# Modulation vectors as sums along rows on VectorE, and four pairs of tiles in the first k loop

## The chip, the cores and the metric

The kernel runs on one core of one Trainium2 chip. The metric is the device time of one execution in microseconds (us), the median over the runs shown. TensorE (PE in the rows), VectorE (DVE), ScalarE (ACT), GpSimd (POOL) and the queue that issues the transfers (SyncE, SP) each work through a stream of their own in order and wait for each other by semaphores.

## The reference, cut to what matters

One block of a network on x of 512 tokens by 1024 features, in float32. A conditioning vector c of 1024 numbers is made into nine vectors of 1024 (shift, scale and gate of three sublayers), the modulation vectors; the sublayers use them. The full reference has a pooled and state-space mixer as its second sublayer, which the change leaves as it is.

```
mod = (silu(c) @ w_ada + b_ada).reshape(1, 3, 3, 1024)     # w_ada: 1024 x 9216
shift, scale, gate = mod[:, :, 0], mod[:, :, 1], mod[:, :, 2]
h = rmsnorm(x, norm_g[0]) * (1 + scale[:, 0]) + shift[:, 0]
x = x + 0.5 * gate[:, 0] * swiglu(h, ffn1_in, ffn1_out)     # a, b = split(h @ w_in); (silu(a) * b) @ w_out
h = rmsnorm(x, norm_g[1]) * (1 + scale[:, 1]) + shift[:, 1]
x = x + gate[:, 1] * hybrid_mixer(h, ...)
h = rmsnorm(x, norm_g[2]) * (1 + scale[:, 2]) + shift[:, 2]
x = x + 0.5 * gate[:, 2] * swiglu(h, ffn2_in, ffn2_out)
return rmsnorm(x, final_g)
```

## The kernel before, in words

Features lie on the 128 partitions: x is 8 tiles (k = 0 to 7) of 128 features by 512 tokens. Every large product runs as three float32r matmuls (`mm3`, L312 to L314): weight and activation are each split into a rounded part and the rest (hi and lo), and hi·hi, hi·lo and lo·hi are added up in one PSUM bank. A weight unit of 128x1024 is eight 128x128 tiles. It is loaded into `w_raw`, ScalarE writes its hi part (L123, `w_hi`), and VectorE the lo part (L126, `w_lo`); five units are held split and three raw, and the splitting runs up to three units ahead of the products.

**Start.** `first_pairs` writes the order of all engines by hand. The transfers of x come first, then the constants `vec`, then the weights in the order of use. ScalarE squares the tiles of x, VectorE adds the squares (L685), TensorE sums them over the partitions (L352), eleven small steps on VectorE make the inverse root per token (L695 to L346), and TensorE spreads it over the partitions (L375, called rs). TensorE fills its idle stretches there with matmuls of ones (L672).

**First k loop.** The first `NSTART` pairs of output tiles of the first layer (three pairs, so six PSUM banks) are summed with k outermost, since the first k can start before the others are ready. Step k needs the modulated tile h[k], as hi and lo, and so scale and shift of sublayer 0 for the 128 features of tile k. They come from w_ada: `ada_load` fetches four tiles of 256 KB for a step, `ada_first` runs eight matmuls of 128x32 by 128x256 in plain float32 (L406), each of which leaves two records, ScalarE copies the rows out (L409), and `ada_turn` turns them with two transposes (L419) and adds and reduces them in three small steps on VectorE (L420 to L425). Then x·rs·gs (L515, into `tmp`), the hi part on ScalarE (L516) and the lo part on VectorE (L517) follow. For k = 0 these are L725, L730, and L731 with L732; the first matmul of the loop is L740.

**Pairs after the loop.** Each later pair is two products of 24 matmuls (k innermost), with silu and product behind them (`glu`, L605 and L607, split at L325 and L327). `ffn` runs the 22 pairs in three portions; after each portion come eight output products of one bank each, which add gate times product to x (L524).

**Other modulation vectors.** The other seven of the nine vectors are made behind the k loop by a generator, `ada_rest`, that `pump` advances six steps per pair and one per output product: 112 steps, each a multiply-add of a 128x512 tile on VectorE (L464, L466); after every eight steps `ada_row` sums over the partitions with four matmuls against ones (L486), ScalarE copies the row, and four small transfers scatter it over the partitions.

After `first_pairs`, TensorE's order is the program's, and the other engines' orders are made by a scheduler.

## Time and profile before

| | |
|---|---|
| median of 3 runs | 1163.68 us (1160.77 to 1164.01) |
| profiled execution | 1160.53 us, of which the span from first to last instruction is 1158.5 us |
| granted TensorE clock, mean over the span | 0.996 of full speed |
| TensorE busy | 1146.2 us, 99% of the span |
| VectorE busy | 629.9 us, 54% |
| ScalarE busy | 396.6 us, 34% |
| GpSimd busy | 119.3 us, 10% |
| moved by transfers | 140.17 MB |

A share is taken over the whole span. Matmuls overlap their neighbours, so a matmul's recorded length is longer than the distance to the next one; in a full stream the distance between starts is what one costs.

### The profile page before, as it was taken

To read this page: it belongs to the slowest core of one execution; us is meant where nothing else is said; L and a number is where in the kernel's file an instruction comes from. 1 tells how busy PE (TensorE), PEld (TensorE's weight loads), DVE (VectorE), ACT (ScalarE), POOL (GpSimd) and SP (SyncE) were. 2 spreads that over 40 slices of the span, in tenths; PEclk is the share of its full clock that TensorE was granted. 3 is DMA by queue.
4 is the path that set the end of the run, shared out by engine and by line. 5 is a ranking of instruction groups with operands and counts; after the bars stand their busy time and mean duration, and the time that the engine had idled before them with its cause. 6 is when DMAs were issued, how large, how long until landed. Compare 5 with 4: busy or idle time off the path is not lost.

```text
span 1158.5 us, 15066 instructions
## 1 busy us (share of the span) xinstructions
PE 1146.2 (99%) x5948; PEld 940.8 (81%) x5948; DVE 629.9 (54%) x975; ACT 396.6 (34%) x660; POOL 119.3 (10%) x122
## 2 busy tenths in 40 slices
PE   8999999999999999999999999999999999999997
PEld 6677787777877997888888878899888888888887
DVE  4567736667363666677968595563333333333334
ACT  4352222221223453454544453343321222212232
POOL 0000000000000320023112561121000000000001
PEclk9999999999999999999999999999999999999999
DMA  9585735756352411222212213440332233323312
GB/s 346 170 293 178 261 115 198 256 190 228 123 178 91 141 60 52 77 73 73 74 55 73 73 56 91 124 131 20 91 91 91 93 103 96 92 91 91 95 33 73
DMA packets 52837, 140.17 MB, mean 121 GB/s; under 512 B 7456, under 2 KB 8864, under 8 KB 52768
## 3 DMA queue, kind: packets, MB, share of 16 engines
q1 hardware_dynamic: 52768, 139.23, 37.1%
q8 instruction: 46, 0.75, 0.3%
q14 instruction: 23, 0.19, 0.1%
HBM read 137.08 MB, written 2.10 MB: 120 GB/s over the span
## 4 chain that ended last, share of the span: by engine, by line
PE 98%; DVE 1%; DMA 0%; ACT 0%; SPq 0%; issue 0%; DVEq 0%; ACTq 0%
PE ps_mm L312 24%; PE ps_mm L313 23%; PE ps_mm L314 23%; PE ps_t L314 6%; PE ps_t L313 6%; PE ps_t L312 6%; PE ps_y L965 1%; PE ps_mm L352 1%; PE ps_mm L406 1%; PE ps_t L959 1%; PE ps_y L984 1%; PE ps_mm L375 1%; PE ps_t L927 0%; DMA x<-in_x_dram 0%; PE ps_t L930 0%; PE ps_t L932 0%
## 5 line engine op out<-in xcount | busy, mean ns | idle before, releaser
L312 PE MATMUL ps_mm<-big,w_hi 128*128 128x512 f32 (+1 forms) x1192 | 454.9, 382 | 0.0
L313 PE MATMUL ps_mm<-big,w_hi 128*128 128x512 f32 (+1 forms) x1192 | 448.1, 376 | 0.1
L314 PE MATMUL ps_mm<-big,w_lo 128*128 128x512 f32 (+1 forms) x1192 | 448.0, 376 | 0.0
L123 ACT CAST w_hi<-w_raw 128x1024 fp32r<-128x1024 f32 (+1 forms) x178 | 185.9, 1045 | 521.3 <-PE ps_mm L313 309.4
L126 DVE TENSOR_TENSOR w_lo<-w_raw,w_hi 128x1024 fp32r<-128x1024 f32 (+1 forms) x178 | 220.8, 1242 | 171.7 <-ACT w_hi L123 160.6
L312 PEld LDWEIGHTS ps_mm<-big,w_hi 128*128 128x128 f32 x1192 | 224.1, 188 | 50.3 <-issue 8.2
L314 PEld LDWEIGHTS ps_mm<-big,w_lo 128*128 128x128 f32 x1192 | 224.1, 188 | 44.8
L313 PEld LDWEIGHTS ps_mm<-big,w_hi 128*128 128x128 f32 x1192 | 224.2, 188 | 43.6 <-issue 0.7
L314 PE MATMUL ps_t<-big,w_lo 128*128 128x512 f32 x312 | 123.4, 396 | 0.0
L312 PE MATMUL ps_t<-big,w_hi 128*128 128x512 f32 x312 | 123.4, 396 | 0.0
L313 PE MATMUL ps_t<-big,w_hi 128*128 128x512 f32 x312 | 123.4, 396 | 0.0
L524 DVE SCALAR_TENSOR_TENSOR x<-ps_mm,mod,x 128x512 f32<-128x512 f32 (+1 forms) x79 | 51.1, 648 | 127.6 <-PE ps_mm L314 127.5
L331 POOL TENSOR_TENSOR sacc<-sacc,sq 128x256 f32<-128x256 f32 (+1 forms) x30 | 28.7, 956 | 747.4 <-ACT sq L386 416.1
L607 DVE TENSOR_TENSOR tmp<-tmp,ps_t 128x512 f32<-128x512 f32 x39 | 26.8, 688 | 104.4 <-PE ps_t L314 104.4
L466 DVE SCALAR_TENSOR_TENSOR big<-big,sc 128x512 f32<-128x512 f32 x98 | 73.6, 751 | 12.6 <-DMA big<-in_ada_dram 10.1
L314 PEld LDWEIGHTS ps_t<-big,w_lo 128*128 128x128 f32 x312 | 58.6, 188 | 14.2
L313 PEld LDWEIGHTS ps_t<-big,w_hi 128*128 128x128 f32 x312 | 58.6, 188 | 14.2
L312 PEld LDWEIGHTS ps_t<-big,w_hi 128*128 128x128 f32 x312 | 58.6, 188 | 14.1
L877 DVE SCALAR_TENSOR_TENSOR big<-ps_mm,vec,big 128x511 f32<-128x511 f32 (+2 forms) x60 | 44.7, 745 | 2.2 <-ACT big L875 1.3
L325 ACT CAST big<-tmp 128x512 fp32r<-128x512 f32 (+1 forms) x66 | 36.5, 556 | 2.0 <-DVE tmp L607 1.4
L312 PE MATMUL ps_mm<-big 128*128 128x256 f32 x128 | 36.5, 286 | 0.0
L313 PE MATMUL ps_mm<-big 128*128 128x256 f32 x128 | 36.2, 283 | 0.0
(179 smaller groups left out, 891.1 us busy)
## 6 DMA issues: line engine op xcount, KB each, us to landing
w_raw<-in_ffn_in_dram SPq DMA_DIRECT2D x78, 512.0 KB, 3.5
big<-in_ada_dram SPq DMA_DIRECT2D x144, 256.0 KB, 4.8
w_raw<-in_ffn_out_dram SPq DMA_DIRECT2D x44, 512.0 KB, 3.8
w_raw<-in_w_in_dram SPq DMA_DIRECT2D x32, 512.0 KB, 3.5
w_raw<-in_w_outB_dram SPq DMA_DIRECT2D x10, 512.0 KB, 3.6
w_raw<-in_w1s_dram SPq DMA_DIRECT2D x8, 384.0 KB, 5.8
w_raw<-in_w_outA_dram SPq DMA_DIRECT2D x6, 512.0 KB, 3.9
x<-in_x_dram SPq DMA_DIRECT2D x8, 256.0 KB, 5.3
```

What stands on the lines that cost most here:

```text
L123: nc.scalar.copy(out=hi[:, :n], in_=r)
L126: nc.vector.tensor_tensor(out=lo[:, :n], in0=r, in1=hi[:, :n].bitcast(F32), op=ALU.subtract)
L312: T.matmul(o, lhsT=hi, rhs=ahi[:, s], start=first, stop=False)
L313: T.matmul(o, lhsT=hi, rhs=alo[:, s], start=False, stop=False)
L314: T.matmul(o, lhsT=lo, rhs=ahi[:, s], start=False, stop=last)
L325: self.nc.scalar.copy(out=hi[:, s], in_=src[:, :n])
L331: self.nc.gpsimd.tensor_tensor(out=acc, in0=acc, in1=q, op=ALU.add)
L352: self.nc.tensor.matmul(ps[:, at + j:at + j + 1], lhsT=acc[:, c * P - c0:(c + 1) * P - c0], rhs=self.ones[:, 0:1], start=i == 0, stop=i == ...
L466: V.scalar_tensor_tensor(out=acc, in0=ws.pop(i), scalar=self.sc[:, q:q + 1], in1=acc, op0=ALU.mult, op1=ALU.add)
L524: self.nc.vector.scalar_tensor_tensor(out=xs, in0=ps[:, :n], scalar=self.mod[:, gate, m:m + 1], in1=xs, op0=ALU.mult, op1=ALU.add)
L607: nc.vector.tensor_tensor(out=g32, in0=sa, in1=pb[:, :n], op=ALU.mult)
L877: V.scalar_tensor_tensor(out=acc[:, s:], in0=ps[:, :NT - s], scalar=tap(3 - s), in1=acc[:, s:], op0=ALU.mult, op1=ALU.add)
```

## The change

All nine modulation vectors are made in one way, without TensorE. The weights w_ada lie transposed in memory, so that a tile `row` of 128x1024 holds, for 128 output features, all 1024 weights of each. c is copied to all partitions (`cb`, 128x1024, 512 KB) and put through silu once. One call of `tensor_tensor_reduce` multiplies a row tile with `cb` and adds up along the row, starts from the bias and scales on the way, so that it leaves 128 finished numbers (`ada_sum`). Four row tiles are held (`NROW`). `ada_first`, `ada_turn` and `ada_row` are gone, and so are the small transfers of `ada_row`. `ada_rest` becomes 56 steps, three per pair and one per output product.

The k loop carries four pairs, which takes all eight PSUM banks; rs, which lay in one of them, is copied to a tile of its own (`rs_sb`) first. Its weight unit grows from 128x768 to 128x1024. In step 0 the order of the matmuls becomes hi·hi for all eight tiles, then lo·hi, then hi·lo. x is loaded, squared and added in tiles of two k. The number of `big` tiles falls from 50 to 48, and the numbers of warming matmuls change.

```diff
-NSTART = 3
+NSTART = 4
-NBIG = 50
+NBIG = 48
-PREADA = 5
-PUMPS = (6, 1)
-WARM = 22
-WARM1 = 0
-WARM2 = 3
-WARM3 = 2
+NROW = 4
+PUMPS = (3, 1)
+WARM = 24
+WARM1 = 7
+WARM2 = 4
...
+    def ada_load(self, j, k):
+        w = self.sb.tile([P, KD * P], F32, name="row", tag="row", bufs=NROW)
+        self.nc.sync.dma_start(out=w, in_=self.a["ada"][j, k])
+        return w
+
+    def ada_sum(self, j, k, w):
+        sub, typ = divmod(j, 3)
+        scale, bias, out = 1.0, self.bada[:, j, k:k + 1], self.mod[:, j, k:k + 1]
+        if typ == 1:
+            scale, bias, out = self.ng[:, sub, k:k + 1], self.gb[:, sub, k:k + 1], self.gs[:, sub, k:k + 1]
+        elif typ == 2 and sub != 1:
+            scale, bias = 0.5, self.hb[:, sub, k:k + 1]
+        self.nc.vector.tensor_tensor_reduce(out=w, in0=w, in1=self.cb, scale=scale, scalar=bias,
+                                            op0=ALU.mult, op1=ALU.add, accum_out=out)
+
+    def ada_rest(self):
+        steps = [(j, k) for j in (2, 4, 3, 5, 7, 6, 8) for k in range(KD)]
+        ws = []
+        for i, (j, k) in enumerate(steps):
+            ws += [self.ada_load(*t) for t in steps[len(ws):i + NROW]]
+            self.ada_sum(j, k, ws[i])
             yield
...
+        def load(k):
+            if k < KD:
+                rows[k] = [self.ada_load(j, k) for j in (1, 0)]
+            self.W.load(k + 1)
...
+        S.activation(out=self.cb, in_=self.cb, func=AF.Silu)
...
+        self.ada_sum(1, 0, rows[0][0])
+        warm(WARM1)
         v, y, t, u = self.root_tiles(NCHK)
...
+        rs = self.spread(y)
+        warm(WARM2)
         h = self.new_h()
+        self.ada_sum(0, 0, rows[0][1])
+        n0, rs_sb = self.tmp(), self.big()
+        V.tensor_tensor(out=n0, in0=self.x[:, 0, :], in1=rs, op=ALU.mult)
...
+        def prepare(k):
+            for j, w in zip((1, 0), rows.pop(k)):
+                self.ada_sum(j, k, w)
+            t, (hi, lo) = self.tmp(), h[k]
+            V.scalar_tensor_tensor(out=t, in0=self.x[:, k, :], scalar=self.gs[:, 0, k:k + 1], in1=rs_sb,
+                                   op0=ALU.mult, op1=ALU.mult)
+            shift = self.mod[:, 0, k:k + 1]
+            S.activation(out=hi, in_=t, func=AF.Identity, bias=shift)
+            return lambda: V.scalar_tensor_tensor(out=lo, in0=t, scalar=shift, in1=hi.bitcast(F32),
+                                                  op0=ALU.add, op1=ALU.subtract)
...
         for k in range(KD):
-            load(k + 3)
+            load(k + 2)
             ws = self.W.take(2 * NSTART)
...
+            else:
+                for w, p in zip(ws, pss):
+                    self.mm3(p, w, h[k], FULL, False, k == KD - 1)
+            if k < KD - 1:
+                rest = []
+                self.W.ensure(k + 2, lambda: rest.append(prepare(k + 1)))
+                rest[0]()
```

In the rows below the names are the program's tiles, and the line numbers are those of each kernel's own file. The first place is TensorE in step k = 1 of the loop. Before, from the modulation matmuls of a later k to the transposes of the next and the matmul behind them (`ps_mm_241` and up are the banks of the pairs):

```order
L406 MATMUL ps_mm_300<-big_201,sc32_81 32x256 x2
L312 MATMUL ps_mm_241<-big_161,w_hi_276 128x512
L313 MATMUL ps_mm_241<-big_162,w_hi_276 128x512
L314 MATMUL ps_mm_241<-big_161,w_lo_277 128x512
L312 MATMUL ps_mm_242<-big_161,w_hi_276 128x512
L313 MATMUL ps_mm_242<-big_162,w_hi_276 128x512
L314 MATMUL ps_mm_242<-big_161,w_lo_277 128x512
L419 MATMUL ps_mm_331<-vec_65,tmp_309 128x128 x2
L312 MATMUL ps_mm_243<-big_161,w_hi_276 128x512
```

The same engine in the changed kernel, from the last bank of step 1 into step 2 (`mm3` is now L310 to L312, `w_hi_284` the unit of step 2):

```order
L310 MATMUL ps_mm_213<-big_179,w_hi_244 128x512
L311 MATMUL ps_mm_213<-big_180,w_hi_244 128x512
L312 MATMUL ps_mm_213<-big_179,w_lo_245 128x512
L310 MATMUL ps_mm_206<-big_181,w_hi_284 128x512
L311 MATMUL ps_mm_206<-big_182,w_hi_284 128x512
L312 MATMUL ps_mm_206<-big_181,w_lo_285 128x512
```

The matmuls of L406 and the transposes of L419 are gone from between the steps; a step is 24 matmuls of one kind where it was 18, with ten more behind and between them.

The second place is VectorE in the loop. Before, what it does for one step:

```order
L126 TENSOR_TENSOR w_lo_277<-w_raw_193,w_hi_276 128x768
L420 TENSOR_REDUCE mod_82<-ps_mm_280 128x2
L422 SCALAR_TENSOR_TENSOR gs_83<-mod_82,vec_65,gb_111 128x1
L425 TENSOR_TENSOR mod_82<-mod_82,vec_65 128x1
L515 SCALAR_TENSOR_TENSOR tmp_286<-x_68,gs_83,ps_mm_219 128x512
L517 SCALAR_TENSOR_TENSOR big_162<-tmp_286,mod_82,big_161 128x512
```

And in the changed kernel (an ISA row of 128x1024 is the product and sum of `ada_sum`, the ISA row of 128x1 behind it reads the result out; L124 splits the weights, `w_raw_118`):

```order
L402 ISA row_114,gs_79<-row_114,cb_73,gb_142,vec_65 128x1024
L402 ISA gs_79 128x1
L402 ISA row_116,mod_78<-row_116,cb_73,vec_65 128x1024
L402 ISA mod_78 128x1
L652 SCALAR_TENSOR_TENSOR tmp_249<-x_68,gs_79,big_195 128x512
L124 TENSOR_TENSOR w_lo_245<-w_raw_118,w_hi_244 128x1024
L656 SCALAR_TENSOR_TENSOR big_180<-tmp_249,mod_78,big_179 128x512
```

Three small steps became two long ones with a read-out each; the split of the weights, a third longer, moved behind x·rs·gs.

The third place is the transfer queue at the start of the program. Before:

```order
L650 DMA x<-in_x_dram 128x512 x8
L651 DMA vec<-in_vec_dram 128x416
L395 DMA big<-in_ada_dram 128x512 x4
L103 DMA w_raw<-in_w1s_dram 128x768
L395 DMA big<-in_ada_dram 128x512 x4
```

And in the changed kernel:

```order
L569 DMA x<-in_x_dram 128x1024 x4
L571 DMA cb<-in_c_dram 128x1024
L572 DMA vec<-in_vec_dram 128x408
L391 DMA row<-in_ada_dram 128x1024 x2
L101 DMA w_raw<-in_w1s_dram 128x1024
```

`cb` stands new between x and `vec`, and the unit of weights behind the two row tiles of step 0 is larger. In the order that the scheduler makes behind the loop, 54 of the 56 sums of `ada_rest` stand between the fourth `glu` product and the twelfth behind it on VectorE; in the same stretch stand 25 splits of weight units (L124), 12 `glu` products with their lo parts, and the 8 additions to x of the first portion. The orders of VectorE, ScalarE and GpSimd in the mixer and behind it are those of before.

## Rows read from the trace of the kernel before

**Rows 1.** The page: busy time of TensorE, and the chain that ended last.

```profile
PE 1146.2 (99%) x5948; PEld 940.8 (81%) x5948; DVE 629.9 (54%) x975; ACT 396.6 (34%) x660; POOL 119.3 (10%) x122
...
PE 98%; DVE 1%; DMA 0%; ACT 0%; SPq 0%; issue 0%; DVEq 0%; ACTq 0%
```

**Rows 2.** Waits of TensorE over the span, the two longest: us, times, longest.

```profile
PE ps_mm L740 <- ACT big L730: 2.0, 1, 2.0
PE ps_mm L352 <- DVE big L685: 1.2, 1, 1.2
```

**Rows 3.** Timeline of TensorE, start and length: loop's start, its end, next pair.

```profile
19.90 0.50 PE L740 MATMUL ps_mm<-big,w_hi 128*128 128x512 f32 x1 [2.03 <-ACT big L730]
...
63.88 0.40 PE L312 MATMUL ps_mm<-big,w_hi 128*128 128x512 f32 x1
...
69.48 0.40 PE L312 MATMUL ps_t<-big,w_hi 128*128 128x512 f32 x1
...
75.08 0.40 PE L312 MATMUL ps_mm<-big,w_hi 128*128 128x512 f32 x1
```

**Rows 4.** Timeline of TensorE in step k = 1.

```profile
26.71 0.50 PE L312 MATMUL ps_mm<-big,w_hi 128*128 128x512 f32 x1
...
31.32 1.07 PE L406 MATMUL ps_mm<-big,sc 128*32 128x256 f32 x16
32.32 0.50 PE L312 MATMUL ps_mm<-big,w_hi 128*128 128x512 f32 x1
```

**Rows 5.** Line L486 over the span, and TensorE's timeline around its first call.

```profile
L486 PE MATMUL ps_y<-big,ones x112: 272/285/297, 97.6 to 351.3; 128*32 128x128 f32 x112
...
97.25 0.40 PE L314 MATMUL ps_t<-big,w_lo 128*128 128x512 f32 x1
...
97.93 0.50 PE L312 MATMUL ps_mm<-big,w_hi 128*128 128x512 f32 x1
98.27 0.40 PE L313 MATMUL ps_mm<-big,w_hi 128*128 128x512 f32 x1
```

**Rows 6.** Groups of VectorE by shape: busy us, mean ns; then its timeline, in a stretch without waits.

```profile
L126 DVE TENSOR_TENSOR w_lo<-w_raw,w_hi 128x1024 fp32r<-128x1024 f32 x170 | 213.1, 1255 | 158.5 <-ACT w_hi L123 149.1 <-PE ps_t L961 1.4
L466 DVE SCALAR_TENSOR_TENSOR big<-big,sc 128x512 f32<-128x512 f32 x98 | 73.6, 751 | 12.6 <-DMA big<-in_ada_dram 10.1
...
87.33 0.75 DVE L466 SCALAR_TENSOR_TENSOR big<-big,sc 128x512 f32<-128x512 f32 x1
87.99 1.22 DVE L126 TENSOR_TENSOR w_lo<-w_raw,w_hi 128x1024 fp32r<-128x1024 f32 x1
89.13 0.69 DVE L327 TENSOR_TENSOR big<-tmp,big 128x512 fp32r<-128x512 f32 x1
89.73 0.75 DVE L466 SCALAR_TENSOR_TENSOR big<-big,sc 128x512 f32<-128x512 f32 x1
```

**Rows 7.** Timelines of VectorE and ScalarE at the start: first and last root step, step 0.

```profile
12.81 0.16 DVE L695 TENSOR_SCALAR root<-ps_mm 128x4 f32<-128x4 f32 x1 [0.98 <-PE ps_mm L352]
...
14.79 0.16 DVE L346 SCALAR_TENSOR_TENSOR root<-root 128x4 f32<-128x4 f32 x1
...
18.31 0.68 DVE L725 TENSOR_TENSOR tmp<-x,ps_mm 128x512 f32<-128x512 f32 x1
...
20.67 0.49 DVE L732 TENSOR_SCALAR big<-tmp,mod 128x512 fp32r<-128x512 f32 x1
...
19.03 0.82 ACT L730 ACTIVATE big<-tmp,mod,gs 128x512 fp32r<-128x512 f32 x1 [1.95 <-DVE tmp L725]
```

**Rows 8.** Stretches: length, busy time by engine, granted clock, DMA share, GB/s.

```profile
2.00:8.00 6.00, 6.00 (x39) 6.00 (x38) 0.69 (x1) 2.72 (x6) 0.00 (x0) 1.00 0.97 292
8.00:18.00 10.00, 7.80 (x58) 5.80 (x56) 5.46 (x19) 4.08 (x9) 0.00 (x0) 0.83 1.05 395
13.00:16.00 3.00, 3.00 (x22) 1.51 (x22) 1.64 (x10) 0.03 (x1) 0.00 (x0) 0.50 1.06 396
18.00:24.00 6.00, 4.10 (x30) 2.70 (x31) 4.11 (x10) 1.93 (x3) 0.00 (x0) 1.00 1.05 390
```

## The prediction, made before the changed kernel was timed

> **What bounds the kernel now.** I read the busy times and the chain first [rows 1]: TensorE is busy for 1146.2 of 1158.5 us, and the chain of work that ended last runs through it for 98% of the span. Then its waits [rows 2]: the longest is 2.0 us, before the first matmul of the k loop, and both that are shown lie in the first 20 us. VectorE, with 54%, is waited for only there. So the time is the sum of what TensorE has to do, plus a start of some 20 us in which it waits for its first operands. What leaves TensorE's stream behind the start is gained in full, as long as no other engine becomes late for it.

> The price of a matmul is read from the distance of starts, not from its length. From 63.88 to 69.48 us a product of 24 matmuls of 128x512 runs [rows 3]: 5.60 us, or 0.2333 us each, though each is recorded with 0.40. The k loop starts at 19.90 and its last matmul is followed by the fourth pair's first at 63.88; that pair, two products, ends at 75.08. So from the loop's start to the end of pair four TensorE takes 55.18 us, of which 4 x 2 x 8 x 3 = 192 matmuls are 44.80.

> **What is removed.** A step of the loop takes from 26.71 to 32.32, 5.61 us, with 18 matmuls, 4.20 us [rows 4]. The other 1.41 us are the modulation matmuls of L406 (start to next start 1.00, and the neighbours' spacing) and the two transposes. Over the loop 43.98 - 33.60 = 10.4 us go to this and to one short wait. All of that leaves TensorE. Behind the loop `ada_row` goes: around its first call the matmul at 97.25 is followed by the next but one, not counting L486, at 98.27, 1.02 us where two spacings are 0.47 [rows 5]. That is 0.555 us a call, and 112 records at two for each of four matmuls are 14 calls: 7.8 us. It is gained whole, because TensorE has no wait in that stretch. The fourth pair's matmuls only move into the loop.

> **What VectorE gets.** The product and sum of 128x1024 is in no row. The nearest is the split of a weight unit, also two float32 streams of 1024 elements out of SBUF: 1.255 us long, and 1.14 from its start to the next one's where nothing is waited for (87.99 to 89.13) [rows 6]. The read-out is a small step; the root's small steps, each behind the last, come every 0.2 us (ten in 1.98) [rows 7]. So a sum costs at least 1.14 us, if its read-out is free, 1.34 with the read-out in sequence, 1.46 if the read-out also waits for the whole length, and at most about 2.5, if product and sum are two passes of 1.14 with a read-out. I take **1.4**, because it is one instruction with the split's operands and output. A step of the loop then holds two sums, x·rs·gs (0.66 us from start to start, as L466 at 87.33), the split 1.14 and the lo part 0.66: 2.8 + 2.46 = **5.26 us**, against 24 x 0.2333 = 5.60 for TensorE. VectorE stays ahead up to a sum of (5.60 - 2.46) / 2 = 1.57 us.

> [...]

> Behind the loop VectorE does 54 sums in a stretch with 25 splits (1.14), 12 glu products with lo parts (0.60 each, as L327 from 89.13 to 89.73) and 8 additions to x (0.66): 28.5 + 14.4 + 5.3 + 54 x 1.4 = 124 us. TensorE spends on the same stretch eight pairs of 11.20 and eight output products of 5.60, 134.4 us. The sums fit, up to 1.6 us each. What waits in VectorE's queue behind a late sum is the next split, and TensorE for that; splits run up to three units, 16.8 us of products, ahead. So the edit to `ada_rest` costs nothing under cover of that slack, and with the cover gone 54 times the excess.

> **The start.** What was ready at 19.90 is ready when? Transfers run at 292 GB/s in the stretch that brings x, later at 395 [rows 8]. At these rates the 2.10 MB of x are in at about 8.9 us. Then `cb` (0.52 MB, 1.3 us), `vec` (0.21, 0.5) and the first row tile (1.3) come, at about 12.1; the second at 13.4, the weights of step 0 at 14.8. In VectorE's order the first sum stands ahead of the root, which is queued behind it: 12.1 + 1.4 = 13.5. The eleven root steps took from 12.81 to 14.95: ready at 15.65. The second sum ends at 17.05; in its cover TensorE spreads rs. Then x·rs 0.68 and the hi part 0.82 [rows 7], with two handovers: first matmul at **18.6**. Bounds: if x too came at 395 GB/s, 1.6 us earlier, 16.9; if the first row tile lands only with the whole group behind it, at 14.8, 21.3. So the start gains 1.3 us (3.0 to -1.4).

> Step 1 then meets a late VectorE: after x·rs at 17.75 come the split (1.14), L731's and L732's successors (0.75, 0.49 [rows 7]), a constant (0.2), two sums (2.8), x·rs·gs, the split and the lo part (0.66, 1.14, 0.75). That ends at 25.65, while TensorE could take the second matmul of step 1 at 18.6 + 5.60 + 0.23 = 24.4. A wait of **1.2 us** is new. From step 2 VectorE gains 0.34 us a step. Transfers: a step needs 1.57 MB in 5.26 us, 300 GB/s, below the 395 seen, and the queue is two steps ahead; hidden.

> [...] ScalarE gets one silu of 128x1024 ahead of the first sum (about as long as a split, ready before the row tile) and the copy of rs to a tile, which the eighth bank's first matmul waits for, 1.6 us after the loop's start; both hidden. Two fewer `big` tiles: the orders in the mixer are unchanged, so nothing.

> **The sum.** Fourth pair done at 18.6 + 44.8 + 1.2 = 64.6 where it was 75.08: 10.5 us. With 7.8 from `ada_row`: **18.3 us** less. The profiled execution took 1160.5 us, its span and 2.0 around it, which gives 1142.2; the median of the runs is 3.2 higher and would give 1145.4. I say **1144**.

> **The rivals.**
> 1. *The start and the first steps eat part of it.* First matmul at 21.3 and the low clock: 18.3 - 2.7 - 1.5 = 14, so 1149 or so. For it speaks `cb` and a sum ahead of the root; against it that w_ada's tiles of step 0 were not what the old start waited for last.
> 2. *VectorE becomes the bound* (the other side). At 2.5 us a sum a step of the loop takes 5.0 + 2.46 = 7.46, 1.86 over TensorE's, seven times: 13. Two sums at the start and two in step 1: 4.4 more. Behind the loop 48.2 + 135 = 183 against 134.4 + 16.8 ahead: 32. In all 49 - 18 = 31 slower, 1193. It decides where the losses reach 18: at a sum of about 2.05 us. For it: the accumulation has no row. [...]
> 3. *In between*, a sum of 1.6 to 2.05 us: part of the gain, 1150 to 1162; at 1.8 us the loop loses 3.2, start and step 1 1.6, and the cover behind takes the rest: 1149.
> 4. *The freed time comes back as waits elsewhere*: transfers (312 GB/s in the output products, with 2 to 3 row tiles each) or a split that stands behind a sum waiting for its row. 1155 to 1165. Against it: the queue has four row tiles and splits are three units ahead.

> **How the numbers follow.** Forecast (1139 to 1148) 0.70, rival 1 0.09, rival 2 0.09, rival 3 0.07, rival 4 0.05. The range 1139 to 1153 holds the forecast, rival 1 and half of rival 3. A difference within 0.3%, 3.5 us, can't be told from none here. Faster takes the forecast, rival 1, most of 3 and some of 4: 0.86. Same: 0.04. Slower: 0.10.

> **What would show it.** In the new profile: the sum's instruction at 1.1 to 1.3 us and its read-out below 0.2; steps of the loop at 5.60 us; loop from about 18.6 to 64.6 with one wait of about 1 us in its second step; no wait of TensorE for VectorE behind it. A sum above 1.6 us, or row tiles on which VectorE waits with TensorE behind it, would make the prediction wrong.

## The result and the profile after

The changed kernel takes 1137.52 us in the median (1137.45 to 1137.97, 4 runs); before, in the same comparison, took 1163.53. The ratio is 0.978 (95% interval 0.9765 to 0.9799): 26.0 us less. The forecast of 1144 had the direction and much of the path right, but the time lies below its range (1139 to 1153), and the gain is 7.7 us larger than the sum of 18.3.

The page of the changed kernel, busy time and the chain that ended last, against [rows 1]:

```profile
PE 1126.4 (99%) x5708; PEld 937.9 (83%) x5708; DVE 635.6 (56%) x969; ACT 391.2 (34%) x632; POOL 117.3 (10%) x122
...
PE 98%; DMA 1%; DVE 1%; SPq 0%; issue 0%; DVEq 0%
```

TensorE still sets the time, with 240 records fewer. Its waits over the whole span, against [rows 2]:

```profile
PE ps_mm L350 <- DVE w_hi L615: 1.3, 1, 1.3
PE ps_mm L591 <- DVE ones L580: 1.1, 1, 1.1
PE ps_mm L373 <- DVE root L344: 0.5, 1, 0.5
```

All three lie in the start; VectorE's 72 sums of 128x1024 have brought no wait behind it. The groups of the new instruction (busy us, mean ns) answer the disputed price:

VectorE's timeline, at the start and in one step of the loop, answers to [rows 6, 7]:

```profile
11.89 1.34 DVE L402 CUSTOM_DVE_ANT_0 row<-row,cb,gb 128x1024 f32<-128x1024 f32 x1 [0.64 <-DMA row<-in_ada_dram]
13.16 0.08 DVE L402 DVE_READ_ACCUMULATOR2_ANT gs<- 128x1 f32 x1
13.16 0.16 DVE L625 TENSOR_SCALAR root<-ps_mm 128x4 f32<-128x4 f32 x1
...
15.14 0.16 DVE L344 SCALAR_TENSOR_TENSOR root<-root 128x4 f32<-128x4 f32 x1
15.22 1.28 DVE L402 CUSTOM_DVE_ANT_0 row<-row,cb,vec 128x1024 f32<-128x1024 f32 x1
...
17.47 0.69 DVE L634 TENSOR_TENSOR tmp<-x,ps_mm 128x512 f32<-128x512 f32 x1 [0.96 <-PE ps_mm L373]
...
25.41 1.34 DVE L402 CUSTOM_DVE_ANT_0 row<-row,cb,gb 128x1024 f32<-128x1024 f32 x1
26.68 0.08 DVE L402 DVE_READ_ACCUMULATOR2_ANT gs<- 128x1 f32 x1
26.68 1.28 DVE L402 CUSTOM_DVE_ANT_0 row<-row,cb,vec 128x1024 f32<-128x1024 f32 x1
...
30.35 1.33 DVE L402 CUSTOM_DVE_ANT_0 row<-row,cb,gb 128x1024 f32<-128x1024 f32 x1
```

Where the next instruction doesn't need its result, a sum is followed by it after 1.2 to 1.27 us: the read-out lies inside that. A step takes 30.35 - 25.41 = 4.94 us. TensorE's timeline in the places of [rows 3]:

```profile
19.06 2.60 PE L667 MATMUL ps_mm<-big,w_hi 128*128 128x512 f32 x8
...
25.20 0.40 PE L310 MATMUL ps_mm<-big,w_hi 128*128 128x512 f32 x1
25.55 0.50 PE L311 MATMUL ps_mm<-big,w_hi 128*128 128x512 f32 x1
...
70.21 0.40 PE L310 MATMUL ps_t<-big,w_hi 128*128 128x512 f32 x1
...
75.81 0.40 PE L310 MATMUL ps_mm<-big,w_hi 128*128 128x512 f32 x1
```

The first product behind the loop ends at 70.21 and takes as long as the second, 5.60, so the four pairs are done at 64.61, where before they were done at 75.08.

Laid side by side, equal matmuls of the two profiled executions stand 10.47 us apart there. At each of the 14 places where `ada_row` was they move 0.555 further apart, to 18.22 behind the last one (352 us in the kernel before). And then, in stretches that the change doesn't touch, the lead grows on: to about 19.0 through the mixer (800 us before) and to 22.18 through the second feed-forward layer. Stretches of 200 us: length, TensorE's busy time and records, clock, DMA share, GB/s. The kernel before:

```profile
860.00:1060.00 200.00, 200.00 (x859) 1.00 0.31 94
```

The changed kernel, in the first feed-forward layer and in the second:

```profile
100.00:300.00 200.00, 200.00 (x859) 1.00 0.56 196
860.00:1060.00 200.00, 200.00 (x867) 1.00 0.30 95
```

No wait, a granted clock of 1.00 in all three, the same instructions: yet 867 matmuls where there were 859. Between starts that is 0.2311 us against 0.2333 (mean of the distances in the stretch), 5.547 us for a product of 24 against 5.600.

### The profile page after: what moved, and what is told of

Its sections match the earlier page's. It is cut to its first block, busy times and chain, and to the rows that moved or that the text cites. A ratio compares the mean times of both kernels' runs of the same rounds, so it can differ in the third digit from the quotient of the medians.

```text
span 1136.2 us, 14273 instructions
## 1 busy us (share of the span) xinstructions
PE 1126.4 (99%) x5708; PEld 937.9 (83%) x5708; DVE 635.6 (56%) x969; ACT 391.2 (34%) x632; POOL 117.3 (10%) x122
## 4 chain that ended last, share of the span: by engine, by line
PE 98%; DMA 1%; DVE 1%; SPq 0%; issue 0%; DVEq 0%
PE ps_mm L311 24%; PE ps_mm L310 24%; PE ps_mm L312 24%; PE ps_t L311 6%; PE ps_t L312 6%; PE ps_t L310 6%; PE ps_y L887 1%; PE ps_mm L373 1%; PE ps_t L881 1%; PE ps_y L906 1%; PE ps_mm L350 1%; DMA row<-in_ada_dram 1%; PE ps_mm L667 1%; PE ps_t L849 0%; PE ps_t L854 0%; PE ps_t L852 0%
## 5 line engine op out<-in xcount | busy, mean ns | idle before, releaser
L310 PE MATMUL ps_mm<-big,w_hi 128*128 128x512 f32 (+1 forms) x1198 | 451.8, 377 | 0.0
L312 PE MATMUL ps_mm<-big,w_lo 128*128 128x512 f32 (+1 forms) x1198 | 450.0, 376 | 0.0
L121 ACT CAST w_hi<-w_raw 128x1024 fp32r<-128x1024 f32 x176 | 185.0, 1052 | 515.2 <-PE ps_mm L311 341.4
L124 DVE TENSOR_TENSOR w_lo<-w_raw,w_hi 128x1024 fp32r<-128x1024 f32 x176 | 220.2, 1252 | 169.4 <-ACT w_hi L121 159.4
L310 PEld LDWEIGHTS ps_mm<-big,w_hi 128*128 128x128 f32 x1198 | 225.1, 188 | 46.9 <-issue 2.9
L312 PEld LDWEIGHTS ps_mm<-big,w_lo 128*128 128x128 f32 x1198 | 224.9, 188 | 42.7
L311 PE MATMUL ps_t<-big,w_hi 128*128 128x512 f32 x304 | 120.2, 395 | 0.0
L312 PE MATMUL ps_t<-big,w_lo 128*128 128x512 f32 x304 | 120.1, 395 | 0.0
L310 PE MATMUL ps_t<-big,w_hi 128*128 128x512 f32 x304 | 119.0, 391 | 0.0
L310 PEld LDWEIGHTS ps_t<-big,w_hi 128*128 128x128 f32 x304 | 57.0, 188 | 14.0
L311 PEld LDWEIGHTS ps_t<-big,w_hi 128*128 128x128 f32 x304 | 57.0, 188 | 13.9
L312 PEld LDWEIGHTS ps_t<-big,w_lo 128*128 128x128 f32 x304 | 57.1, 188 | 12.7
L402 DVE CUSTOM_DVE_ANT_0 row<-row,cb,vec 128x1024 f32<-128x1024 f32 x32 | 40.3, 1279 | 2.7 <-DMA row<-in_ada_dram 2.7
L310 PE MATMUL ps_mm<-big 128*128 128x256 f32 x128 | 36.5, 285 | 0.0
```

Of the source, the lines that this page charges most:

```text
L121: nc.scalar.copy(out=hi[:, :n], in_=r)
L124: nc.vector.tensor_tensor(out=lo[:, :n], in0=r, in1=hi[:, :n].bitcast(F32), op=ALU.subtract)
L310: T.matmul(o, lhsT=hi, rhs=ahi[:, s], start=first, stop=False)
L311: T.matmul(o, lhsT=hi, rhs=alo[:, s], start=False, stop=False)
L312: T.matmul(o, lhsT=lo, rhs=ahi[:, s], start=False, stop=last)
L402: self.nc.vector.tensor_tensor_reduce(out=w, in0=w, in1=self.cb, scale=scale, scalar=bias, op0=ALU.mult, op1=ALU.add, accum_out=out)
```

## The experiments

Every run stood beside runs of the kernel before on the same chip, which took 1161.96 to 1163.32 us in the median.

**The sum's price and VectorE's cover.** Three sums per step in `prepare`; the extra one leaves the shift vector other than the reference's:

```diff
             self.ada_sum(j, k, w)
+            self.ada_sum(0, k, w)
```

> The changed kernel with three sums in place of two in each step k = 1 to 7 of the first loop; the third repeats the shift's on the tile that the second has overwritten, so shift of sublayer 0 is wrong for those tiles. My reading (VectorE is covered as long as a step of it is below TensorE's 5.60 us): a sum measured 1.24 from start to start, a step is 4.94 us, with a third one 6.18: VectorE becomes the bound, the loop's end moves from 64.6 to about 69.2, 4.6 us more than the changed kernel, 1142, and TensorE waits about 0.6 us for VectorE in each step. Rival: the steps have slack elsewhere (splits ahead), less than 2 us more.

1144.8 us (1144.11 to 1145.13), 7.3 more than the changed kernel, and more than expected: TensorE's clock fell once more, to a granted clock of 0.50 from 27.9 to 31.3 us (matmuls start 0.43 us apart there and 0.23 behind it). VectorE's steps take 6.26 us, and TensorE now waits for it inside the loop:

```profile
27.54 1.34 DVE L402 CUSTOM_DVE_ANT_0 row<-row,cb,gb 128x1024 f32<-128x1024 f32 x1
...
33.80 1.34 DVE L402 CUSTOM_DVE_ANT_0 row<-row,cb,gb 128x1024 f32<-128x1024 f32 x1
```

```profile
PE ps_mm L311 <- DVE big L657: 2.0, 5, 0.5
PE ps_mm L310 <- ACT big L656: 1.6, 2, 1.0
```

So VectorE sets the loop here, 6.26 us a step where TensorE's 24 matmuls take 5.60. From the other side, with `NSTART = 3` TensorE's step shrinks to 18 matmuls, 4.20 us:

> The changed kernel with three pairs in the k loop (a smaller unit of weights, 128x768, in it). By the prediction's count a step of VectorE is two sums of 1.24, x times rs times gs 0.66, the split 0.86 and the lo part about 0.75, 4.7 us, against 18 matmuls, 4.20 us: VectorE ends last, seven steps lose 0.45 us each and step 1 some 1.4 more, about 4.5 us: 1142. Rival (VectorE gains enough lead or the fourth pair pays it back): 1137.5.

1141.34 us (1139.73 to 1142.91), 3.8 more. VectorE's step is 4.68 us (29.37 to 34.05), and TensorE's waits again name it:

```profile
PE ps_mm L311 <- DVE big L656: 1.7, 7, 0.3
```

Behind the loop, each of the 56 sums twice (the second adds up the products, so the vectors aren't the reference's):

```diff
             self.ada_sum(j, k, ws[i])
+            self.ada_sum(j, k, ws[i])
```

> The changed kernel with each of the 56 sums behind the loop made twice, the second from the overwritten tile, so the modulation vectors of sublayers 1 and 2 and the first gate are wrong. My reading: VectorE has 134 us in the stretch and needs 48 + 54 x 1.24 = 115; with 108 sums 182, so the order, if it were kept, would cost 182 - 134 - 17 = 31 us; the scheduler may spread the sums over more pairs, since the whole first layer has 270 us, and then the price is smaller. 5 to 31 us more than the changed kernel, with waits of TensorE for splits or for the first gate. Rival: nothing (below 2 us), which would say that the sums had far more cover than I counted.

1138.17 us (1134.07 to 1138.98): nothing. The scheduler spread the sums until 276 us instead of 193; the cover is far larger than the 134 us that the prediction counted.

**What `ada_row` cost.** Its matmuls taken out of the kernel before, the copy reading `acc` instead; the sum over the partitions is left out:

```diff
-        for i in range(4):
-            nc.tensor.matmul(ps[32 * i:32 * (i + 1), 0:P], lhsT=self.ones[:, 0:32], ...)
...
-        nc.scalar.copy(out=row[:, 0:P], in_=ps[:, 0:P])
+        nc.scalar.copy(out=row[:, 0:P], in_=acc[:, 0:P])
```

> The kernel before without the 56 matmuls of ada_row: the row is copied from the accumulated tile itself, so the sum over the partitions is left out and the modulation vectors but shift and scale of sublayer 0 are wrong. My term: 7.8 us less than the kernel before, from TensorE alone, 14 calls of 0.555; the copies on ScalarE and the small transfers stay. Rival: TensorE waits elsewhere for part of it, 0 to 5 us less. By Theory R the distances in later stretches may change as well, and add up to 4 us either way; the time at the first matmul behind the last call tells the term by itself.

1156.05 us, ratio 0.9936 (0.9921 to 0.9951): 6.3 less than before by the medians. Its profiled execution started late (loop done at 66.95), which hides part of the gain. Beside `b_scratch` below, which started as late (66.69), its matmuls are 0.27 us behind at the loop's end and 7.44 ahead at the end of the program: 7.7 us gained.

**The kernel before, once more, and the start.**

> The kernel before, unchanged, profiled once more. Theory R (rhythm): the 3 us between this kernel's runs at 1160.8 and at 1163.5 are a change in the distance between matmul starts in some stretch, with the same instructions; if this execution takes about 1163.5, its profile shows some stretch in which products of 24 matmuls take more than 5.60 us or in which TensorE runs otherwise than in the first profile, and no new wait. Rival W: a wait or a late transfer at the start makes the 3 us; then the first matmul of the k loop stands 3 us after 19.9. If it takes 1160.5 the profile repeats the first within 0.3 us and nothing is told apart.

1162.19 us (1159.93 to 1163.88, 10 runs). All distances are those of the first trace; the loop starts at 20.4 instead of 19.90 and ends 2.0 us later. So what differs is neither a distance in a later stretch nor a wait, but the clock. The two executions (columns as above), first this one, then the one behind the prediction:

```profile
12.00:18.00 6.00, 5.78 (x43) 0.72 1.05 396
18.00:25.00 7.00, 4.97 (x28) 0.76 1.05 392
```

```profile
12.00:18.00 6.00, 5.87 (x43) 0.72 1.05 391
18.00:25.00 7.00, 5.10 (x34) 1.00 1.05 391
```

Here the loop's first microseconds ran partly at a lower clock (0.76 granted from 18 to 25 us), there they didn't (1.00).

More warming matmuls for the changed kernel (`WARM` 24 to 28):

> The changed kernel with 28 warming matmuls at the start in place of 24, nothing else moved behind the first 11 us. Theory R: the phase in which TensorE enters later stretches changes, so the distance in the second feed-forward layer may be 0.2333 again (time up to 4 us longer, 1141.5) though no tile moves. Rival P: 0.2311 stays. For the start: if the sparse stretch between 9.2 and 10.5 us is what lowers the granted clock from 13.3 to 20.1 us, the clock stays high, the spread of rs takes 1.0 instead of 2.1 us and the loop starts at 18.1 instead of 19.1: 1 us less, 1136.5. If the clock falls anyway, start and time stay.

1137.57 us (1135.73 to 1138.96). The start is no faster (loop from 20.06): the clock fell anyway, and earlier (0.50 from 12 to 18 us). But the profiled execution, the one of 1135.73, has 0.2311 in the first feed-forward layer too, though no tile has moved. So at these places the first layer can have either distance; what picks one, no run shows.

**What sets 0.2311 or 0.2333: not a disturbance.** One 128x128 matmul of ones ahead of the second feed-forward layer, in each kernel:

```diff
+        ps = self.bank()
+        self.nc.tensor.matmul(ps[:, 0:P], lhsT=self.ones, rhs=self.ones, start=True, stop=True)
```

> The kernel before with one matmul of ones by ones (128x128, read by nobody) put into TensorE's stream just ahead of the second feed-forward layer's pairs; no tile of the others moves. Theory R (the distance between matmul starts is a state that the stream keeps until something disturbs it): the distance behind it may change from 0.2333 to 0.2311 us, 1160 to 1158 in place of 1162, or stay. Rival P (the places of the tiles): it stays at 0.2333 and the time is that of before plus 0.3 us.

> The changed kernel with the same extra matmul ahead of the second feed-forward layer. Theory R: the distance behind it may change from 0.2311 to 0.2333 us, some 3 us more, 1140.5, or stay. Rival P: 0.2311 stays, 1137.8. If neither of the two kernels with the extra matmul changes its distance, Theory R loses its mechanism and the distance in that layer is tied to the program.

1162.67 and 1139.43 us; before keeps 0.2333, the changed kernel 0.2311, so Theory R loses its mechanism. (The 1.9 us over the changed kernel come mostly from the start: in this profile the loop ends 1.2 us later.) A smaller reserve at the foot of SBUF moves all tiles of the kernel before by 15,360 bytes:

```diff
-    nc = bacc.Bacc("TRN2", target_bir_lowering=False, num_devices=1)
+    nc = bacc.Bacc("TRN2", target_bir_lowering=False, num_devices=1, dynamic_dma_scratch_size=1024)
```

> The kernel before with the 1024-byte scratch for descriptors of the changed kernel and nothing else, which moves tiles in the on-chip memory and no instruction. In the changed kernel the matmuls of the second feed-forward layer start every 0.2311 us, before every 0.2333, some 4 us in all. Theory R (the rhythm is a state of TensorE's stream): 0.2333 here too, time same as before, 1160.5 to 1164. Rival P (the places of the tiles make the rhythm): another distance than 0.2333 in some stretch and a time 2 us or more off.

1163.37 us (ratio 1.0002), 0.2333: a common shift by 30 x 512 bytes changes nothing, and Rival P fell in this form.

**Where the tiles lie.** A place is a tile's first byte in its partition, as the program assigns it. Tiles of x (`big`) are 2048 bytes, the slices of a weight unit 512, so modulo 512 all of one kind lie alike. The next kernels move them by unused bytes alone; the order of every engine stays.

```diff
         self.gb = sb.tile([P, KD], F32, name="gb")
+        sb.tile([P, 8], F32, name="pad")
```

This is `b_al64`; `b_al128` has 24 there and `b_al512` 56. In the changed kernel the pads are these (`a_al128`), with 8, 24 and, behind `rs_sb`, 8 in `a_al32`, 112 and 16 in `a_al256`; `a_x64` has 16 ahead of `rows` and 16 behind `rs_sb`:

```diff
+        sb.tile([P, 16], F32, name="pad")
         rows = {}
...
         self.hb = sb.tile([P, 3, KD], F32, name="hb")
+        sb.tile([P, 16], F32, name="pad1")
```

> Before, with 32 unused bytes ahead of the weight tiles: w_raw, w_hi and w_lo lie at a multiple of 64 bytes as in the changed kernel, where before they lie 32 bytes off it; the order of every engine and all other work stay. Theory A (the place of the split weights sets the distance of matmul starts): 0.2311 us instead of 0.2333 in the second feed-forward layer, so about 4 us less than before, 1158.3; up to 7 less where the first layer takes it too. Rival S (the distance comes from the changed program: its orders, its number of instructions, how the layer is entered): 0.2333 everywhere, 1162.3.

> The changed kernel, with unused bytes between its tiles so that w_hi and w_lo lie 32 bytes off a multiple of 64, as before; x's split tiles stay at a multiple of 128 and all orders stay. Theory A: 0.2333 us between matmul starts in the second layer as before, 1137.5 + 4.05 = 1141.6. Rival S: 0.2311 there, 1137.5.

> The changed kernel with w_hi, too, at a multiple of 128 bytes (it lies 64 off, w_lo at a multiple). Theory A in the form that 64 bytes are what matters: as the changed kernel, 1137.5, 0.2333 in the first layer and 0.2311 in the second. If 128 bytes matter: 0.2311 in both layers, about 3 us less, 1134.5. Rival S: 1137.5.

Theory A fell as it was put: `b_al64` gained nothing, and `a_al32` became faster where it should have slowed. And `a_al128` went to 1120.1, which no theory had forecast. Rival S fell with that, because nothing but places had changed.

> Before, with 96 unused bytes ahead of the weight tiles, so that w_hi and w_lo lie at a multiple of 128 bytes, as x's split tiles do. Theory W (the weights' place in 128 bytes sets the distance): 0.2267 us in both feed-forward layers as in the changed kernel so placed; 3942 matmuls of 512 columns gain up to 6.6 ns each, 26 us, some less in the mixer: 1139. Against the changed kernel so placed (1120.1) that leaves 19 us for the change itself, near the 18.3 of the prediction's sum. Rival X (the weights have to lie as x's tiles do modulo 512 bytes, which they do there and not here): 0.2333 or 0.2311, 1155 or more.

> The changed kernel with w_hi and w_lo at a multiple of 128 bytes, and x's split tiles (big) moved to 64 bytes off one. Theory W: 0.2267 and 1120.1, as with x's tiles at a multiple of 128. Rival X (both sides' places count, or their distance): 0.2311 to 0.2333, 1133 to 1142.

Theory W fell: weights at a multiple of 128 aren't enough. Of the tiles that these matmuls read, `a_x64` moves only x's against `a_al128`, and takes 20 us more.

> Before, with 224 unused bytes ahead of the weight tiles: w_hi, w_lo and x's split tiles all lie at 384 modulo 512 bytes, as in the one kernel with 0.2267 us. Theory X (equal places modulo 512 on both sides): 0.2267 in both feed-forward layers, 1162.8 - 23 = 1140, and 20 us more than the changed kernel so placed (1120.1). If something else of the changed kernel is needed for 0.2267: 1155 or more.

> The changed kernel with w_hi, w_lo and x's split tiles all at 256 modulo 512 bytes. Theory X (equal places, wherever): 0.2267, 1120. If the place itself counts (384): 0.2311 or more, 1133 to 1142.

Theory X stands. All nine, with the places of x's tiles, `w_hi` and `w_lo` modulo 512, the mean distance of starts in the first and second feed-forward layer (200 to 340, without the places of `ada_row`, and 860 to 1080 us), and the median:

| kernel | x | w_hi | w_lo | first, us | second, us | median, us |
|---|---|---|---|---|---|---|
| before | 384 | 160 | 160 | 0.2333 | 0.2333 | 1163.53 |
| b_al64 | 384 | 192 | 192 | 0.2334 | 0.2333 | 1162.31 |
| b_al128 | 384 | 256 | 256 | 0.2326 | 0.2324 | 1159.95 |
| b_al512 | 384 | 384 | 384 | 0.2270 | 0.2267 | 1139.59 |
| after | 256 | 320 | 256 | 0.2333 | 0.2311 | 1137.52 |
| a_x64 | 320 | 384 | 384 | 0.2333 | 0.2333 | 1140.50 |
| a_al32 | 384 | 352 | 416 | 0.2311 | 0.2311 | 1133.58 |
| a_al128 | 384 | 384 | 384 | 0.2267 | 0.2267 | 1120.10 |
| a_al256 | 256 | 256 | 256 | 0.2267 | 0.2267 | 1119.32 |

The second layer in `b_al512`, the old program with 224 unused bytes, by the stretch that held 859 matmuls before; then in `a_al128` and in `a_x64`:

```profile
860.00:1060.00 200.00, 200.00 (x884) 1.00 0.32 98
```

```profile
860.00:1060.00 200.00, 200.00 (x884) 1.00 0.30 97
```

```profile
860.00:1060.00 200.00, 200.00 (x859) 1.00 0.30 93
```

`a_al256` beats both kernels: 0.9633 of before (0.9616 to 0.9649), 18 us under the change as it was made.

## Why the prediction was right, and where it failed

- **What bounds the kernel** was right: TensorE's stream (98% of the chain that ended last), and what left it was gained whole (7.75 us for `ada_row`, 7.8 counted).
- **The sum**, predicted at 1.4 us, takes 1.2 to 1.27 from start to start; a step of VectorE 4.94 instead of 5.26. That it is one pass was right: the instruction is 1.28 us long with two float32 sources and an accumulation, beside 1.25 for the split with as many elements. `a_loop3` and `a_n3` show that the comparison of the two engines' steps was the right one: TensorE waited for VectorE in the loop at 6.26 us a step against 5.60 and at 4.68 against 4.20. Rivals 2 and 3 fell with that price.
- **The start** was right to half a microsecond: row tile at 11.8 (12.1 predicted), last root step at 15.30 (15.65), first matmul at 19.06 (18.6). The spreading of rs took 2.08 us at a granted clock of 0.50, longer than the sum that was to cover it: 0.96 us of waiting on VectorE. Rival 1 would have had the first matmul at 21.3. (The early bound, 18.6 - 1.6, is 17.0 and not 16.9; nothing hangs on it.)
- **The new wait in step 1** (1.2 us) is only 0.12: step 0 ran partly at a granted clock of 0.50 (to 20 us) and took 6.14 us instead of 5.60, so VectorE was nearly in time. A start 0.46 us later and 0.54 us of low clock stand where the wait of 1.2 was to be, and the loop's end, 64.6, came out to the tenth. The 1.5 us that rival 1 takes off for a low clock are in no row; this trace shows the 0.54, and `b_again`, whose loop starts 0.5 us later than that of [rows 3] and ends 2.0 later, 1.5 with the old start. The agreement is luck: other traces of this start (`a_warm28`, `a_sum2`, `a_kick`) end the loop at 65.3 to 65.8.
- **`ada_row`**: 18.22 - 10.47 = 7.75 us between the traces, 7.7 in `b_norow`, 7.8 predicted.
- **The stretch behind the loop** has more cover than counted; no loss, as predicted, and none of rival 4's waits.
- **The step that failed** is the price of a matmul, 0.2333 us, which the prediction carried over from the old layout for the whole program; where it looked at the tiles it said "Two fewer `big` tiles: the orders in the mixer are unchanged, so nothing." The orders are unchanged; the places are not. The two `big` tiles move nothing modulo 512, since each has 2048 bytes, but new tiles and other sizes moved x's tiles from 384 to 256 and the weights from 160 to 320 and 256. The changed kernel's matmuls behind the last `ada_row` then took less, 0.2311 in the second feed-forward layer: 22.18 - 18.22 = 3.96 us that no term held. Without them the time would have been 1141.5, inside the range. That the places do it and not the changed program is shown by `a_x64`, the same program at other places, which has 0.2333 in that layer again. `a_al32`, `a_x64` and `a_al128` show that such places are worth from 3 us of loss to 17 of gain.
- **The base of the sum** is the rest. The profiled execution of before (1160.5 us) was 3.0 under its median because its loop started at a granted clock of 1.00; the prediction saw the gap of 3.2 and put its number in between. The two profiled executions differ by 22.56 us, 0.4 of it outside these matmuls; 3.0 and, on the side of the changed kernel, 0.45 make it 26.0. In seven traces of the old start at about 0.2333 us a matmul, two have a granted clock of 1.00 from the loop's first matmul on and end it at 63.4 (`b_kick`) and 63.9; the five others ran at a lower one for part of 20 to 25 us (0.66 in the mean there) and end it at 65.9 to 67.0. For the runs without a trace it is argued.

At equal places the change is worth about what the prediction said, where its sum is 18.3: `b_al512` against `a_al128`, 1139.59 - 1120.10 = 19.5 us, and against `a_al256`, which ran on the same chip, 20.3. The profiles of `b_al512` and `a_al128` show its terms without the growth: equal matmuls stand 10.5 us apart at the loop's end, 18.1 behind the last `ada_row`, and still 18.3 at 1100 us.

## What to carry to other kernels

Before you price an edit that changes tiles, look at where the operands of the engine that sets the time will lie: here 224 unused bytes gave the old kernel 22 us, more than the change is worth at equal places. A matmul's price holds for one layout (0.2267 to 0.2334 us in the nine here), so take its distance again from a stretch that the edit doesn't touch before you explain a gain by the edit. And make a sum against several executions: one profile can be a lucky start (here 3.0 us under the median).

## What the runs showed that was not expected

Matmuls of 128x512 in float32r, each with a weight load of its own, start every 0.2267 us where the places of moving tile and weights agree modulo 512 bytes (all three kernels with such places: at 384 and at 256, in both programs), and on average every 0.231 to 0.233 us in the six layouts where they don't, at a granted clock of 1.00 and without waits. That is 2 to 3% of TensorE's time. One kind of weights alone doesn't bring it: in the changed kernel `w_lo` agrees with x's tiles (256) and `w_hi` doesn't (320), and the distances are 0.2333 and 0.2311. In the second layer every single distance is 0.226 or 0.227 at equal places; in the kernel before they go from 0.231 to 0.235, in the changed kernel from 0.225 to 0.236. Differences by multiples of 512, which the slices of one unit have among them, show in none of the distances at equal places. At the changed kernel's places both 0.2333 (five traces) and 0.2311 (`a_warm28`) occur in the first layer. Why the places count, whether a difference of 256 would do, and what picks the distance in a layout with two of them stays open.
